# Low parts of the recurrence's weights, its query-decay products and partial sums of two norms: VectorE in place of GpSimd

## The chip, the cores and the metric

One core of a Trainium2 chip runs the whole program. The metric is the device time of one execution in microseconds (us); of several runs the median counts. Engines: PE is TensorE (matrix products, transposes), ACT is ScalarE, DVE is VectorE, POOL is GpSimd, SP issues most of the DMAs. Each engine works through its own instructions in program order, and waits on semaphores for what another engine makes.

## The reference

A streaming encoder with two layers: layer 0 has a pooling mixer, layer 1 an HGRN2 recurrence, and each is followed by a convolutional feed-forward network (FFN); a last norm ends it. It runs on a prompt of 1024 rows and on 64 rows of a running stream, with a width of 1024, 8 heads of 128 and an FFN width of 2816.

```python
def trunk(...):
    for i in range(DEPTH):                    # DEPTH = 2
        hn = rmsnorm(x, norm_mix_g[i])
        if i % 2 == 0: y, st = pool_mix(hn, ...)
        else:          y, st = hgrn_mix(hn, S0, w_in, lb, gn, w_out)
        x = x + y
        hn = rmsnorm(x, norm_ffn_g[i])
        y, cs = conv_ffn(hn, ...)             # w_up, 3-tap conv, silu(gate) * val, w_down
        x = x + y
    x = rmsnorm(x, norm_out_g)

# inside hgrn_mix, per head: zq, zf, zi, zg = split(h @ w_in)
q, k, log_f = silu(zq), (1 - lb) * sigmoid(-zf), ...     # f = exp(log_f), the decay per channel
S_new = exp(bC) * S + k_decayed^T v                      # state 128 x 128
o = (q * exp(b)) S + A v                                 # A: decayed q k products, causal
o = rmsnorm(o) * silu(zg);  y = o @ w_out
```

All of it is fp32.

## The kernel before, in words

**Layout.** The state x lies in SBUF with the 1024 channels as 8 tiles of 128 partitions, tokens along the free axis. The tokens are worked in three chunks of 384, 384 and 320 columns (256 of the prompt and the 64 of the other stream).

**Products.** An fp32 product is made of three passes of a rounded format (fp32r): hi times hi, hi times lo, lo times hi (`mm3`, L180 to L182). So each operand is split: the high part is a ScalarE cast, the low part is source minus high part, one `tensor_tensor` subtraction. For activations that is `split` (L185 ACT, L186 the engine that the caller names).

**Weights.** `load_ready` takes the next 128x512 block of a hand-written queue as soon as a slot of the weight pool is free: a DMA on SP's queue into one of the raw buffers, the ScalarE cast (L128) into `whi...`, the subtraction (L129, GpSimd) into `wlo...`. The phase in the queue is "f" for the FFNs and "g" for the recurrence; "g" has 64 blocks of w_in (`in`, head, projection, half) and 16 of w_out (`out`). Some of the blocks of "g" lie in a spare buffer that appears as `wx` in the trace. Blocks of the up projections are sums and differences of raw blocks, made on VectorE (L152).

**Norms.** `norm(c, gbase, nm, kind)` serves all of them: kind 0 is the norm ahead of FFN 0 (tiles `_x`), 1 the one ahead of the recurrence (`_m`), 2 the one ahead of FFN 1 (`_f`), 3 the last (`_o`). For each of the 8 channel tiles d ScalarE squares it; from d = 2 on the square is added to one of two partial sums, `acc0` for even d and `acc1` for odd d (L366). L373 adds the two, PE transposes (L378, `nps_`), VectorE reduces, `rstd` makes the reciprocal root by Newton steps on 128x3 values (L333 to L344, tile `nt_`), PE spreads it over the rows (L391, `nr_`), and per channel tile L417 scales and `split` makes `hnhi` and `hnlo`.

**Recurrence.** For each head and chunk four projections (`pj`, L180 to L182) make q, k and f, v, and the gate; `core` then makes qq = q times f (L915) and runs three levels of products over blocks of 4, 16 and 64 tokens: VectorE multiplies q and k by decays (L936, called at L938, L939 and L947 to L951), PE multiplies (L945, `pl`), VectorE copies under a mask into `at` (L960). Then come the states (L998), the head's norm and gate (tile `nt_g`), and the output projection `op`, which is added to x at L1049.

**Order.** PE's order is set by a hand-written scheduler in the kernel: tasks that are generators and yield the PE time and a latency (constants N_..., LAT_...). On the other engines the order follows from a list scheduler of the framework, which places instructions by its own estimate of when they are ready. Each engine then keeps that order.

Of the kernel before, what the change touches and what calls it, by code (L numbers as in the profile page):

```python
# [9 lines left out]
F32 = mybir.dt.float32  # L10
# [55 lines left out]
def trunk_kernel(ctx: ExitStack, tc: tile.TileContext, xtok, xs_tok, hist_tok, xf, par, gmix, pw, winm, ident_in,  # L66
# [39 lines left out]
    free = [(i, False) for i in range(NR)]  # L106
    extra_w = []

    def load_ready(most=None):

        while queue and (most is None or len(loaded) < most):
            ph, key, make = queue[0]
            own = [p for p in free if p[1]] if ph == "g" and key[:2] not in (("out", H - 2), ("out", H - 1)) else []
            p = own[0] if own else next((p for p in free if not p[1]), None)
            if p is None:
                return
            free.remove(p)
            queue.pop(0)
            places[key] = p
            i, extra = p  # L120
            nm = "_".join(str(k) for k in key)
            if extra:
                hi, lo = (extra_w[i // 2][:, (i % 2 * 2 + b) * HW_:(i % 2 * 2 + b + 1) * HW_] for b in range(2))
            else:
                hi = wp.tile([P, HW_], F32R, name=f"whi{nm}", tag=f"whi{i}", bufs=1)
                lo = wp.tile([P, HW_], F32R, name=f"wlo{nm}", tag=f"wlo{i}", bufs=1)
            src = make(nm)
            nc.scalar.copy(hi, src)  # L128
            nc.gpsimd.tensor_tensor(lo, src, hi.bitcast(F32), op=ALU.subtract)  # L129
            loaded[key] = (hi, lo)  # L130

    def raw_block(nm, src, i):
# [220 lines left out]
    def norm(c, gbase, nm, kind):  # L353
# [5 lines left out]
        for d in range(ND):  # L359
            a = acc[d % 2][:, :n]  # L360
            if d < 2:
                nc.scalar.activation(a, x[c][:, d, :], AF.Square)
            else:
                sq = slot(f"sq_{nm}{d}", *tags[2:])
                last = nc.scalar.activation(sq[:, :n], x[c][:, d, :], AF.Square)
                (nc.vector if kind == 0 or final and c == 2 or d % 2 else nc.gpsimd).tensor_tensor(a, a, sq[:, :n], op=ALU.add)  # L366
        if final:
            with tc.issue_after(last.ins):
                for d in range(ND):
# [31 lines left out]
        for d in range(ND):  # L401
            if final:
                on_pool = c < 2 or d in (2, 5)
                eng, r_ = (nc.gpsimd, rs) if on_pool else (nc.vector, pr)
                eng.tensor_tensor(x[c][:, d, :], x[c][:, d, :], r_[:, :n], op=ALU.mult)

                if c < 2 and d % 2 or c == 2 and (d % 2 == 0 or d == ND - 1):
                    d0 = d - (0 < d and (c < 2 or d % 2 == 0))
                    nc.sync.dma_start(y_out[c][:, d0:d + 1, :], x[c][:, d0:d + 1, :])
            else:  # L410
                if kind == 2 and c < 2 or kind == 0 and c == 1:
                    t = row(kind // 2, c, d)
                elif kind == 0 and c < 2:
                    t = slot(f"hn_{nm}{d}", ("hh1", "hl1")[d % 2], 2, F32, NMAX)
                else:
                    t = slot(f"hn_{nm}{d}", "cv", 3)
                last = nc.vector.scalar_tensor_tensor(t[:, :n], x[c][:, d, :], col(gbase, d), pr[:, :n], op0=ALU.mult, op1=ALU.mult)  # L417
                split(hn_hi[c][:, d, :], hn_lo[c][:, d, :], t[:, :n], (nc.vector, nc.gpsimd)[d % 2 and kind == 1])
                if d < ND - 1:
                    yield 0.0, N_STEP[kind]  # L420
        return last.ins
# [448 lines left out]
    def core(h, c, pr, stage):  # L870
# [41 lines left out]


        qq, q = qt[:, :n], qt[:, NMAX:NMAX + n]
        nc.gpsimd.tensor_tensor(qq, q, f[:, :n], op=ALU.mult)  # L915
        p0 = prod(kk, q, f"pl{nm}_d")
        nc.vector.tensor_tensor(at[:, :so].rearrange("p (b t) -> p b t", t=P), p0[:, :so].rearrange("p (b t) -> p b t", t=P),
                                ident.unsqueeze(1).to_broadcast([P, full, P]), op=ALU.mult)
# [261 lines left out]
```

## Time and profile before

| | |
|---|---|
| median of 3 runs | 2372.37 us (2372.25 to 2373.45) |
| the profiled execution | 2377.06 us |
| its span in the trace | 2375.2 us |
| mean granted PE clock over the span | 0.98 of full speed |

The profile is of one execution of its own, which took 4.7 us more than the median; its span is 1.9 us shorter than its time. Start times in rows count from the start of the span. FFN 0 ends at about 890 us, the recurrence runs from about 860 to 1580 us, FFN 1 begins at about 1525 us; the stretches overlap, since the three chunks follow one another.

### The profile page before, as it was taken

Reading aid. Unit: us, or ns where it says so; the run is one execution under the profiler, and the core shown is the slowest. Engines: PE = TensorE matmul, PEld = TensorE weight load, DVE = VectorE, ACT = ScalarE, POOL = GpSimd, SP = SyncE. Lnnn points to the kernel's source line nnn. Section 1 sums busy time; section 2 is a strip of 40 time slices with the busy share of each in tenths; the row PEclk is TensorE's granted clock in tenths of the full one; section 3 lists DMA queues with packets and bytes.
Section 4 is the critical chain, followed back from the end, with each engine's and each line's share of the span. In section 5 each row is a group of like instructions: output and inputs, shape, how many; then the busy total and the mean of one; then the engine's idle time right before and its main releaser. Section 6 shows DMA issues by size and latency. Waiting matters only on the chain. (4 is left out here: it accounts for less than half of the span.)

```text
span 2375.2 us, 38111 instructions
## 1 busy us (share of the span) xinstructions
PE 2284.7 (96%) x13830; PEld 2231.3 (94%) x13830; DVE 1613.8 (68%) x3728; ACT 904.3 (38%) x1965; POOL 1003.0 (42%) x1054
## 2 busy tenths in 40 slices
PE   9889999999999989999999999889999999999996
PEld 8889999999999989999999999878999999999996
DVE  6786656566666688767667767778766666666567
ACT  5444333334433353323323322345333333443335
POOL 1155554556655562112112211224454555564555
PEclk8999999999999999999999999989999999999998
DMA  7123333333433321001011000102343334433431
GB/s 233 49 81 116 125 121 120 123 125 129 138 116 125 124 69 36 26 18 54 26 35 40 32 26 22 36 25 76 111 130 116 125 119 134 134 124 117 129 120 76
DMA packets 118099, 218.70 MB, mean 92 GB/s; under 512 B 13436, under 2 KB 17404, under 8 KB 117528
## 3 DMA queue, kind: packets, MB, share of 16 engines
q1 hardware_dynamic: 117822, 216.15, 28.0%
q8 instruction: 109, 1.79, 0.3%
q14 instruction: 78, 0.64, 0.1%
q10 hardware_dynamic: 90, 0.12, 0.0%
HBM read 210.51 MB, written 5.72 MB: 91 GB/s over the span
## 5 line engine op out<-in xcount | busy, mean ns | idle before, releaser
L129 POOL TENSOR_TENSOR wloup_a<-rawup_a,whiup_a 128x512 fp32r<-128x512 f32 x368 | 513.1, 1411 | 568.1 <-ACT whiup_a L128 534.4
L128 ACT CAST whiup_a<-rawup_a 128x512 fp32r<-128x512 f32 x368 | 224.2, 617 | 573.8 <-PE dn L181 397.4
L152 DVE TENSOR_TENSOR rawup_a<-rawup_a,rawup_a 128x512 f32<-128x512 f32 x200 | 186.6, 933 | 286.4 <-DMA rawup_a<-w_up_in 261.4
L180 PE MATMUL dn<-hh,whidn 128*128 128x384 f32 (+1 forms) x1056 | 351.5, 333 | 11.5 <-DVE x L757 8.0
L181 PE MATMUL dn<-hl,whidn 128*128 128x384 f32 (+1 forms) x1056 | 348.7, 330 | 0.7 <-DVE hl L186 0.7
L182 PE MATMUL dn<-hh,wlodn 128*128 128x384 f32 (+1 forms) x1056 | 348.9, 330 | 0.0
L757 DVE TENSOR_TENSOR x<-x,dn 128x384 f32<-128x384 f32 (+1 forms) x528 | 262.3, 528 | 97.1 <-PE dn L182 95.5
L180 PEld LDWEIGHTS dn<-hh,whidn 128*128 128x128 f32 x1056 | 200.2, 190 | 18.0 <-DVE x L757 13.4
L181 PEld LDWEIGHTS dn<-hl,whidn 128*128 128x128 f32 x1056 | 200.1, 190 | 1.3 <-DVE hl L186 1.3
L182 PEld LDWEIGHTS dn<-hh,wlodn 128*128 128x128 f32 x1056 | 200.1, 189 | 0.0
L180 PE MATMUL pj<-hnhi,whiin 128*128 128x384 f32 (+1 forms) x528 | 185.0, 350 | 1.1 <-ACT hnhi L185 1.1
L181 PE MATMUL pj<-hnlo,whiin 128*128 128x384 f32 (+1 forms) x528 | 173.0, 328 | 2.4 <-POOL hnlo L186 2.4
L182 PE MATMUL pj<-hnhi,wloin 128*128 128x384 f32 (+1 forms) x528 | 173.2, 328 | 0.0
L630 DVE SCALAR_TENSOR_TENSOR cv<-ge,prm,cv 128x322 f32<-128x322 f32 (+1 forms) x132 | 132.1, 1002 | 48.2 <-ACT cv L629 42.0
L129 POOL TENSOR_TENSOR wlodn<-rawdn,whidn 128x512 fp32r<-128x512 f32 x88 | 119.0, 1354 | 100.9 <-ACT whidn L128 76.8
L960 DVE COPY_PREDICATED at<-masks,pl 128x64 f32<-128x64 uint8 (+7 forms) x432 | 117.0, 293 | 50.5 <-PE pl L945 48.8
L632 ACT ACTIVATE cv<-cv 128x322 f32<-128x322 f32 (+1 forms) x132 | 67.2, 509 | 161.3 <-DVE cv L631 160.9
L180 PE MATMUL pv<-hnhi,whiup_a 128*128 128x320 f32 (+1 forms) x384 | 122.1, 318 | 0.0
L180 PE MATMUL pg<-hnhi,whiup_a 128*128 128x320 f32 (+1 forms) x384 | 122.1, 318 | 0.0
L182 PE MATMUL pg<-hnhi,wloup_a 128*128 128x320 f32 (+1 forms) x384 | 121.7, 317 | 0.0
L182 PE MATMUL pv<-hnhi,wloup_a 128*128 128x320 f32 (+1 forms) x384 | 121.5, 317 | 0.0
L181 PE MATMUL pg<-hnlo,whiup_a 128*128 128x320 f32 (+1 forms) x384 | 121.5, 316 | 0.0
(1234 smaller groups left out, 6199.0 us busy)
## 6 DMA issues: line engine op xcount, KB each, us to landing
rawup_a<-w_up_in SPq DMA_DIRECT2D x568, 256.0 KB, 2.8
rawdn<-w_dn_in SPq DMA_DIRECT2D x88, 256.0 KB, 3.1
rawin<-w_in_in SPq DMA_DIRECT2D x64, 256.0 KB, 2.6
rawupp_a<-w_up_in SPq DMA_DIRECT2D x16, 256.0 KB, 2.7
rawout<-w_out_in SPq DMA_DIRECT2D x16, 256.0 KB, 2.7
xt<-xtok_in SPq DMA_DIRECT2D x7, 448.0 KB, 6.7
x<-xf_in SPq DMA_DIRECT2D x2, 1536.0 KB, 8.7
y_out<-x SPq DMA_DIRECT2D x8, 384.0 KB, 2.3
```

The costliest lines, as they stand in the source:

```text
L128: nc.scalar.copy(hi, src)
L129: nc.gpsimd.tensor_tensor(lo, src, hi.bitcast(F32), op=ALU.subtract)
L152: nc.vector.tensor_tensor(t[0], t[0], t[1], op=bs[2])
L180: nc.tensor.matmul(ps, w[0][:, wsl], a_hi, start=first, stop=False, skip_group_check=more)
L181: nc.tensor.matmul(ps, w[0][:, wsl], a_lo, start=False, stop=False, skip_group_check=more)
L182: nc.tensor.matmul(ps, w[1][:, wsl], a_hi, start=False, stop=last, skip_group_check=more)
L630: nc.vector.scalar_tensor_tensor(t[:, :wd], ge[:, 0:wd], prm[:, cw[0]:cw[0] + 1], t[:, :wd], op0=ALU.mult, op1=ALU.add)
L632: nc.scalar.activation(t[:, :wd], t[:, :wd], AF.Silu)
L757: nc.vector.tensor_tensor(x[c][:, d, :], x[c][:, d, :], pd[:, :n], op=ALU.add)
L960: nc.vector.copy_predicated(dst[:, :, :, d * hh:], mk, a)
```

## The change

Four kinds of GpSimd instructions become VectorE instructions, with the same operands:

- the low parts (L129) of the weights of phase "g", 80 subtractions of 128x512, by a new helper `lo_engine(ph, key)`;
- the even partial sums of the norms of kind 1 and 2 (L366), 18 additions; the last norm keeps 6 of its own on GpSimd;
- the low parts of the odd channel tiles of the norm of kind 1 (L418), 12 subtractions;
- qq (L915), 24 products.

```diff
--- before.py
+++ after.py
@@ -105,6 +105,9 @@
     places = {}
     free = [(i, False) for i in range(NR)]
     extra_w = []
+
+    def lo_engine(ph, key):
+        return nc.vector if ph == "g" else nc.gpsimd
 
     def load_ready(most=None):
 
@@ -126,7 +129,7 @@
                 lo = wp.tile([P, HW_], F32R, name=f"wlo{nm}", tag=f"wlo{i}", bufs=1)
             src = make(nm)
             nc.scalar.copy(hi, src)
-            nc.gpsimd.tensor_tensor(lo, src, hi.bitcast(F32), op=ALU.subtract)
+            lo_engine(ph, key).tensor_tensor(lo, src, hi.bitcast(F32), op=ALU.subtract)
             loaded[key] = (hi, lo)
 
     def raw_block(nm, src, i):
@@ -363,7 +366,7 @@
             else:
                 sq = slot(f"sq_{nm}{d}", *tags[2:])
                 last = nc.scalar.activation(sq[:, :n], x[c][:, d, :], AF.Square)
-                (nc.vector if kind == 0 or final and c == 2 or d % 2 else nc.gpsimd).tensor_tensor(a, a, sq[:, :n], op=ALU.add)
+                (nc.vector if kind < 3 or c == 2 or d % 2 else nc.gpsimd).tensor_tensor(a, a, sq[:, :n], op=ALU.add)
         if final:
             with tc.issue_after(last.ins):
                 for d in range(ND):
@@ -415,7 +418,7 @@
                 else:
                     t = slot(f"hn_{nm}{d}", "cv", 3)
                 last = nc.vector.scalar_tensor_tensor(t[:, :n], x[c][:, d, :], col(gbase, d), pr[:, :n], op0=ALU.mult, op1=ALU.mult)
-                split(hn_hi[c][:, d, :], hn_lo[c][:, d, :], t[:, :n], (nc.vector, nc.gpsimd)[d % 2 and kind == 1])
+                split(hn_hi[c][:, d, :], hn_lo[c][:, d, :], t[:, :n], nc.vector)
                 if d < ND - 1:
                     yield 0.0, N_STEP[kind]
         return last.ins
@@ -912,7 +915,7 @@
 
 
         qq, q = qt[:, :n], qt[:, NMAX:NMAX + n]
-        nc.gpsimd.tensor_tensor(qq, q, f[:, :n], op=ALU.mult)
+        nc.vector.tensor_tensor(qq, q, f[:, :n], op=ALU.mult)
         p0 = prod(kk, q, f"pl{nm}_d")
         nc.vector.tensor_tensor(at[:, :so].rearrange("p (b t) -> p b t", t=P), p0[:, :so].rearrange("p (b t) -> p b t", t=P),
                                 ident.unsqueeze(1).to_broadcast([P, full, P]), op=ALU.mult)
```

The order of PE's instructions is the same, row by row. VectorE has 134 rows of it more and GpSimd 134 fewer. The list scheduler also moves some of the other VectorE instructions. From L108 on a line of the changed kernel has a number that is 3 higher (L129 becomes L132, L186 becomes L189, L366 becomes L369, L417 becomes L420).

**At the border from FFN 0 to the recurrence.** VectorE before, around the norm of the second chunk; `nt_m` are the Newton steps, `hn_m` the scaled rows, `cv` and `hl` belong to FFN 0:

```order
L344 SCALAR_TENSOR_TENSOR nt_m_9105<-nt_m_9105 128x3
L186 TENSOR_TENSOR hl_20_2_9177<-hr_20_2_9173,hh_20_2_9176 128x320
L417 SCALAR_TENSOR_TENSOR hn_m_9213<-x_94,prm,nr_m_9209 128x384
L186 TENSOR_TENSOR hnlo_100<-hn_m_9213,hnhi_97 128x384
L417 SCALAR_TENSOR_TENSOR hn_m_9247<-x_94,prm,nr_m_9209 128x384
L417 SCALAR_TENSOR_TENSOR hn_m_9269<-x_94,prm,nr_m_9209 128x384
L630 SCALAR_TENSOR_TENSOR cv_21_2_9233<-ge_21_2_9226,prm,cv_21_2_9233 128x322
L631 SCALAR_TENSOR_TENSOR cv_21_2_9233<-ge_21_2_9226,prm,cv_21_2_9233 128x322
L186 TENSOR_TENSOR hnlo_100<-hn_m_9269,hnhi_97 128x384
```

GpSimd before, in the same place, where `wloin` and `wx` are low parts of weights of the recurrence:

```order
L129 TENSOR_TENSOR wloin_0_0_9195<-rawin_0_0_9196,whiin_0_0_9194 128x512
L129 TENSOR_TENSOR wx_9329<-rawin_2_0_9332,wx_9329 128x512
L129 TENSOR_TENSOR wloin_0_1_9221<-rawin_0_1_9222,whiin_0_1_9220 128x512
L624 COPY ncv_92<-ge_21_2_9226 128x2
L625 COPY ncv_92<-ge_21_2_9226 128x2
L129 TENSOR_TENSOR wx_9329<-rawin_2_1_9336,wx_9329 128x512
L129 TENSOR_TENSOR wloin_1_0_9255<-rawin_1_0_9256,whiin_1_0_9254 128x512
L186 TENSOR_TENSOR hnlo_100<-hn_m_9247,hnhi_97 128x384
L129 TENSOR_TENSOR wloin_1_1_9277<-rawin_1_1_9278,whiin_1_1_9276 128x512
L129 TENSOR_TENSOR wx_9330<-rawin_3_0_9340,wx_9330 128x512
```

VectorE of the changed kernel, in the same place:

```order
L347 SCALAR_TENSOR_TENSOR nt_m_9105<-nt_m_9105 128x3
L132 TENSOR_TENSOR wloin_0_0_9195<-rawin_0_0_9196,whiin_0_0_9194 128x512
L420 SCALAR_TENSOR_TENSOR hn_m_9213<-x_94,prm,nr_m_9209 128x384
L132 TENSOR_TENSOR wloin_0_1_9221<-rawin_0_1_9222,whiin_0_1_9220 128x512
L189 TENSOR_TENSOR hnlo_100<-hn_m_9213,hnhi_97 128x384
L420 SCALAR_TENSOR_TENSOR hn_m_9247<-x_94,prm,nr_m_9209 128x384
L420 SCALAR_TENSOR_TENSOR hn_m_9269<-x_94,prm,nr_m_9209 128x384
L633 SCALAR_TENSOR_TENSOR cv_21_2_9233<-ge_21_2_9226,prm,cv_21_2_9233 128x322
L189 TENSOR_TENSOR hnlo_100<-hn_m_9247,hnhi_97 128x384
L634 SCALAR_TENSOR_TENSOR cv_21_2_9233<-ge_21_2_9226,prm,cv_21_2_9233 128x322
L132 TENSOR_TENSOR wloin_1_0_9255<-rawin_1_0_9256,whiin_1_0_9254 128x512
L189 TENSOR_TENSOR hnlo_100<-hn_m_9269,hnhi_97 128x384
```

The low parts of the weights now stand between the Newton steps, the scaled rows and the low parts of the rows, and those of the odd rows stand behind their own L420 and no longer behind three subtractions of weights on GpSimd.

**In the second chunk's product levels.** VectorE before, head 2; `at` is the masked copy, `q` and `k` the level products (head 3's q is in the same queue under another number):

```order
L960 COPY_PREDICATED at_1_11673<-masks,pl_1_0_2_11700 128x32x3
L936 TENSOR_TENSOR q__11445<-q__11445,tp_1_11674 128x24x8
L960 COPY_PREDICATED at_1_11673<-masks,pl_1_0_2_11700 128x32x2
L936 TENSOR_TENSOR q__11445<-q__11445,tp_1_11674 128x24x4
L960 COPY_PREDICATED at_1_11673<-masks,pl_1_0_2_11700 128x32
L960 COPY_PREDICATED at_1_11673<-masks,pl_1_1_0_11757 128x16x12
L936 TENSOR_TENSOR q__11445<-q__11445,tp_1_11674 128x24x4 x3
L936 TENSOR_TENSOR k__11634<-k__11634,tp_1_11674 128x48x4
L960 COPY_PREDICATED at_1_11673<-masks,pl_1_1_0_11757 128x16x8
L936 TENSOR_TENSOR k__11634<-k__11634,tp_1_11674 128x24x8
```

And of the changed kernel:

```order
L963 COPY_PREDICATED at_1_11673<-masks,pl_1_0_2_11700 128x32x3
L939 TENSOR_TENSOR q__11445<-q__11445,tp_1_11674 128x24x8
L963 COPY_PREDICATED at_1_11673<-masks,pl_1_0_2_11700 128x32x2
L939 TENSOR_TENSOR q__11445<-q__11445,tp_1_11674 128x24x4
L963 COPY_PREDICATED at_1_11673<-masks,pl_1_0_2_11700 128x32
L132 TENSOR_TENSOR wloin_2_0_11772<-rawin_2_0_11773,whiin_2_0_11771 128x512
L963 COPY_PREDICATED at_1_11673<-masks,pl_1_1_0_11757 128x16x12
L939 TENSOR_TENSOR q__11445<-q__11445,tp_1_11674 128x24x4 x3
L939 TENSOR_TENSOR k__11634<-k__11634,tp_1_11674 128x48x4
L963 COPY_PREDICATED at_1_11673<-masks,pl_1_1_0_11757 128x16x8
L939 TENSOR_TENSOR k__11634<-k__11634,tp_1_11674 128x24x8
```

The subtraction for block 2_0 of w_in stands between two masked copies, behind the two q products of this level and ahead of the copies and products of the next.

**At the border from the recurrence to FFN 1.** VectorE before; `acc_f`, `sq_f` and `row1w` belong to the norm ahead of FFN 1, `states` and `nt_g` to the last head:

```order
L976 TENSOR_TENSOR k__16198<-k__16198,tp_2_16399 128x2x64
L366 TENSOR_TENSOR acc_f_16626<-acc_f_16626,sq_f_16632 128x384
L417 SCALAR_TENSOR_TENSOR row1w_16524<-x_94,prm,nr_f_16520 128x384
L366 TENSOR_TENSOR acc_f_16626<-acc_f_16626,sq_f_16638 128x384
L417 SCALAR_TENSOR_TENSOR row1w_16524<-x_94,prm,nr_f_16520 128x384
L366 TENSOR_TENSOR acc_f_16626<-acc_f_16626,sq_f_16644 128x384
L186 TENSOR_TENSOR hnlo_100<-row1w_16524,hnhi_97 128x384 x2
L417 SCALAR_TENSOR_TENSOR row1w_16575<-x_94,prm,nr_f_16520 128x384
L998 SCALAR_TENSOR_TENSOR states<-states,tp_2_16399,pu_2_16663 128x128
L417 SCALAR_TENSOR_TENSOR row1w_16575<-x_94,prm,nr_f_16520 128x384
L186 TENSOR_TENSOR hnlo_100<-row1w_16575,hnhi_97 128x384
L998 SCALAR_TENSOR_TENSOR states<-states,tp_2_16399,pu_2_16663 128x128
```

And of the changed kernel:

```order
L979 TENSOR_TENSOR k__16198<-k__16198,tp_2_16399 128x2x64
L369 TENSOR_TENSOR acc_f_16625<-acc_f_16625,sq_f_16629 128x384
L369 TENSOR_TENSOR acc_f_16626<-acc_f_16626,sq_f_16632 128x384
L369 TENSOR_TENSOR acc_f_16625<-acc_f_16625,sq_f_16635 128x384
L369 TENSOR_TENSOR acc_f_16626<-acc_f_16626,sq_f_16638 128x384
L369 TENSOR_TENSOR acc_f_16625<-acc_f_16625,sq_f_16641 128x384
L369 TENSOR_TENSOR acc_f_16626<-acc_f_16626,sq_f_16644 128x384
L420 SCALAR_TENSOR_TENSOR row1w_16524<-x_94,prm,nr_f_16520 128x384 x2
L420 SCALAR_TENSOR_TENSOR row1w_16575<-x_94,prm,nr_f_16520 128x384
L189 TENSOR_TENSOR hnlo_100<-row1w_16524,hnhi_97 128x384 x2
L189 TENSOR_TENSOR hnlo_100<-row1w_16575,hnhi_97 128x384
L1001 SCALAR_TENSOR_TENSOR states<-states,tp_2_16399,pu_2_16663 128x128
```

The six partial sums of the norm (three of them from GpSimd) now stand in a row, behind the k product of the last level and ahead of the four L420 rows, two of which stood between the sums before. Further on, L376, which adds the two partial sums, stands ahead of the first Newton step of the gate (L336) in place of behind it.

## Rows read from the trace of the kernel before

**Rows 1.** The page's first part: busy time, share of the span, instructions.

```profile
PE 2284.7 (96%) x13830; PEld 2231.3 (94%) x13830; DVE 1613.8 (68%) x3728; ACT 904.3 (38%) x1965; POOL 1003.0 (42%) x1054
```

**Rows 2.** Windows: length, busy time per engine, granted clock, DMA share, GB/s.

```profile
840.00:900.00 60.00, 50.55 (x283) 48.02 (x282) 52.12 (x122) 29.52 (x60) 35.41 (x31) 0.91 0.18 59
960.00:1020.00 60.00, 60.00 (x390) 58.15 (x389) 41.47 (x158) 18.48 (x56) 10.23 (x11) 1.00 0.08 26
1500.00:1560.00 60.00, 48.53 (x281) 44.41 (x279) 49.38 (x148) 23.17 (x56) 17.75 (x15) 0.89 0.12 36
1560.00:1620.00 60.00, 54.77 (x289) 52.18 (x290) 46.08 (x116) 27.69 (x61) 11.12 (x19) 0.89 0.09 29
1740.00:1800.00 60.00, 60.00 (x365) 60.00 (x364) 36.50 (x56) 25.42 (x50) 37.43 (x40) 1.00 0.40 130
```

**Rows 3.** Waits of PE, 840 to 1700 us: total, times, longest.

```profile
PE pl L945 <- DVE q__16127 L936: 7.3, 2, 3.9
PE nr_m L391 <- DVE nt_m L344: 3.5, 2, 2.3
PE pl L972 <- DVE k__16198 L936: 2.6, 1, 2.6
PE pj L181 <- POOL hnlo L186: 2.4, 1, 2.4
PE nps_f L378 <- DVE acc_f L373: 1.6, 1, 1.6
PE pl L945 <- DVE q__9504 L936: 1.6, 1, 1.6
PE pl L972 <- DVE k__14156 L936: 1.5, 1, 1.5
PE pl L945 <- DVE q__11445 L936: 1.3, 1, 1.3
```

**Rows 4.** Groups of GpSimd instructions, 840 to 1700 us: busy, mean ns, idle before.

```profile
L129 POOL TENSOR_TENSOR wloin<-rawin,whiin 128x512 fp32r<-128x512 f32 x44 | 58.1, 1324 | 111.1 <-ACT whiin L128 105.7 <-DVE at L960 3.1 <-DVE k__9766 L936 1.8
```

**Rows 5.** Timelines of GpSimd and VectorE in a head: start, length, instruction, idle before.

```profile
1091.00 1.26 POOL L129 TENSOR_TENSOR wloin<-rawin,whiin 128x512 fp32r<-128x512 f32 x1 [9.78 <-ACT whiin L128]
1091.08 1.29 DVE L936 TENSOR_TENSOR q__11445<-q__11445,tp 128x96 f32<-128x96 f32 x1
1063.19 0.25 DVE L936 TENSOR_TENSOR q__11132<-q__11132,tp 128x96 f32<-128x96 f32 x1
```

**Rows 6.** Timeline of VectorE at the start of FFN 1: three undisturbed instructions.

```profile
1580.87 0.55 DVE L186 TENSOR_TENSOR hnlo<-row1q,hnhi 128x384 fp32r<-128x384 f32 x1
...
1598.29 0.49 DVE L373 TENSOR_TENSOR acc_f<-acc_f,acc_f 128x320 f32<-128x320 f32 x1
1598.70 0.68 DVE L152 TENSOR_TENSOR rawup_a<-rawup_a,rawup_a 128x512 f32<-128x512 f32 x1
```

**Rows 7.** Timelines of VectorE and GpSimd, first border.

```profile
857.61 1.39 DVE L630 SCALAR_TENSOR_TENSOR cv<-ge,prm,cv 128x322 f32<-128x322 f32 x1 [0.54 <-ACT cv L629]
...
860.08 1.24 POOL L186 TENSOR_TENSOR hnlo<-hn_m,hnhi 128x384 fp32r<-128x384 f32 x1
...
864.38 1.25 DVE L334 TENSOR_SCALAR nt_m<-nt_m 128x3 int32<-128x3 int32 x1
...
872.32 0.90 DVE L343 TENSOR_TENSOR nt_m<-nt_m 128x3 f32<-128x3 f32 x1
...
892.52 0.95 DVE L343 TENSOR_TENSOR nt_m<-nt_m 128x3 f32<-128x3 f32 x1
```

**Rows 8.** Timelines of VectorE and GpSimd, last border.

```profile
1527.21 1.23 DVE L340 TENSOR_TENSOR nt_g<-nt_g 128x3 f32<-128x3 f32 x1
...
1550.93 1.00 POOL L366 TENSOR_TENSOR acc_f<-acc_f,sq_f 128x384 f32<-128x384 f32 x1 [11.73 <-ACT sq_f L365]
...
1551.08 1.26 DVE L186 TENSOR_TENSOR hnlo<-row1w,hnhi 128x384 fp32r<-128x384 f32 x1
...
1557.35 1.02 DVE L936 TENSOR_TENSOR k__16198<-k__16198,tp 128x160 f32<-128x160 f32 x1
```

## The prediction

> **What bounds the kernel now.** I read the page's busy times first [rows 1]: PE is busy in 96% of the span, GpSimd in 42%, VectorE in 68%. So the change takes work from an engine with room and gives it to one with less, and it can gain only where PE stands idle. The windows say where that is [rows 2]. In a window of FFN 1 (1740 to 1800 us) PE is busy for 60.00 of 60 us, in one inside the recurrence (960 to 1020 us) as well. At the two borders it isn't: 50.55 in 840 to 900 us, 48.53 in 1500 to 1560, 54.77 in 1560 to 1620. In the first two of these VectorE is busy for 52.12 and 49.38 us, and the granted clock is 0.91 and 0.89. The waits of PE between 840 and 1700 us [rows 3] name VectorE nearly everywhere: level products (q, k), Newton steps (nt_m), the last sum of a norm (acc_f); one is for a low part from GpSimd (2.4 us). Nothing outside this stretch has an edited instruction in front of a waiting PE.
>
> The reader is to see next why VectorE is late. In head 1 of the second chunk a product of 128x96 takes 1.29 us where the same product in the head before takes 0.25 [rows 5]; the long one starts 0.08 us after a GpSimd subtraction of 1.26 us and ends with it. So a VectorE instruction that meets a GpSimd subtraction lasts as long as that subtraction. The same holds at the borders: a Newton step on 128x3 takes 1.25, 0.90 and 0.95 us [rows 7] and 1.23 [rows 8], a low part of 128x384 1.26 [rows 8] where 0.55 is its undisturbed time [rows 6]. GpSimd's work does not run beside VectorE's at these places; it holds it up.
>
> The Trainium skill, "SBUF — State Buffer", section "Who interferes with whom", says that a VectorE instruction with two SBUF inputs contends with a GpSimd instruction that reads SBUF, and that one with a single SBUF input outside the two-port modes does not. The trace agrees for the products; L334 with its one input, 1.25 us, would have to be in such a mode, which no row here shows. Were single-input steps not freed, place 1 below would keep 1.1 us more.
>
> **The price on VectorE.** A subtraction of 128x512 lasts 0.68 us, one of 128x384 0.55 [rows 6]. Instructions overlap in the pipeline: the 0.49 us sum at 1598.29 has a successor at 1598.70, 0.08 us before its end [rows 6]. So each costs the engine about 0.60, 0.47 and 0.41 us. The moved work is 80 x 0.60 + (12 + 18 + 24) x 0.47 = 73 us, against some 1.3 us each on GpSimd for the subtractions of weights [rows 4]. VectorE's busy time grows by these 73 less the stretches that go. The trace doesn't show these subtractions on VectorE; bounds are 0.55 (the 128x384 row) and 0.68.
>
> **Place 1, the border from FFN 0 (850 to 895 us).** Six Newton steps from 864.38 to 872.32 us sum to 5.2 us (the first and the last of them are in [rows 7]); undisturbed ones in the same chain take 0.16, so 4.2 us of stretch. Other VectorE rows that met GpSimd, from 857.61 to 892.52 us (nine; 1.39 and 0.95 the outermost), hold another 7.5 us. Given back: 11.7 us. Added in the same stretch: 12 subtractions of weights x 0.60, 8 of rows x 0.47, 3 sums x 0.41, one qq, together 12.7 us. So VectorE is as full as it was. What changes is the order. The odd rows' low part no longer stands behind the subtractions of weights on GpSimd (1.24 us long, at 860.08, and PE waited 2.4 us for one of them) [rows 3, 7]; in VectorE's order it stands behind its own scaled row and another row's, and one subtraction of a weight (0.60) ahead. I take 1.5 us off that wait. Of the 3.5 us of waits for nt_m I take 1.5 off: the chain loses 4.2 us of stretch, but subtractions of weights and rows (four to six at 0.5) come between its steps. Against it, 1.0 for the weights that now stand ahead of the even rows' low parts, of which PE takes one each 0.9 us or so. Sum -2.0; bounds -7.0 (both waits go) and +1.0 (only the new work counts).
>
> **Place 2, the heads (900 to 1500 us).** Three even heads of the second chunk have the collision of [rows 5] with a PE wait of 1.3 us each behind it (q__11445, and two more like it) [rows 3]. 1.04 us of each is stretch: 1.29 less 0.25. In the changed order the subtraction stands behind the q products, so PE gets them in time: -3.1 us. The wait for k__14156, 1.5 us [rows 3], ends 1.0 earlier by the same reason. The 68 other subtractions and 24 qq of the recurrence lie in windows where PE has no idle time and VectorE 18 us in 60 [rows 2]; they cost nothing while that room lasts. If the cover is gone, one subtraction costs PE its 0.60 us. In front of the next level's chain stands one in each of some 7 heads: bounds 0 and 4.2, I take +1.0, near the lower end, as the level chains ran without a PE wait in most heads with stretches of 1.04 in them. Sum -3.1.
>
> **Place 3, the border to FFN 1 (1522 to 1572 us).** Of five stretched gate steps, 1.23 us the longest [rows 8], three lay under sums on GpSimd and become short: taken at 0.9, as the last two of [rows 7], less 0.16, that is 2.2 us. Two lay under subtractions for FFN 1, which stay on GpSimd. Three sums of 0.47 are added on VectorE: -0.8. For k__16198 PE waits 2.6 us [rows 3]; the chain had three stretches of 0.7 us (1551.08, 1557.35, and one between) [rows 8], and the sums now stand behind it: -2.1 at best, but the masked copies and output projections around it arrive by PE's own pace, so I take -1.1. For the norm's final sum PE waits 1.6 us [rows 3]; it moves ahead of the gate's steps: -1.2. The six sums in a row wait for ScalarE's squares, and the scaled rows behind them: +0.5, bounds 0 and 2.5. Sum -2.6. The largest wait, 7.3 us for q__16127 [rows 3], is mostly the chain of the last head and has nothing left to hide it; I leave it but for the -0.8.
>
> **Sum.** -2.0 - 3.1 - 2.6 = -7.7 us. Against the profiled execution of 2377.1 us that is 2369.4; that run stood 4.7 us above the median of 2372.4, so by the median the forecast is 2364.7 us. PE's half-clock stretches are taken as they are.
>
> **Rivals.**
> - *VectorE waits for ScalarE (slower).* VectorE works in order. On GpSimd the subtractions waited 105.7 us in all for ScalarE's casts, 2.4 us each over 44 [rows 4], and nothing stood behind them. On VectorE such a wait holds the level products behind it. The casts wait in turn for a slot that PE frees. Where the list scheduler put a subtraction too early, PE loses about 1.3 us, as it now does behind a stretched q [rows 3]. Six of the 80 cancel the gain (6 x 1.3 = 7.8); twelve give 2364.7 + 15.6 = 2380. For it: 2.4 us of wait per subtraction. Against it: in the one place looked at closely, the subtraction stands behind the products that PE waits for, and the cast is done long before (GpSimd ran it 9.78 us after its last work, at once when the cast ended [rows 5], in a stretch without haste for the weight).
> - *The exchange comes out even (no change).* VectorE's stretches go and its own work fills the same time: 11.7 against 12.7 us at place 1. Then only the heads gain, and place 1 and place 3 give nothing: -3.1 and +1 or so, 2370 to 2374. The Trainium skill, "Perfetto Trace Analysis", section "Optimizing Scalar/DVE Operations", has it this way: GpSimd and VectorE share a read port, so moving work between them might not help. By that rule the time would stay at about 2372.
> - *The clock gains too.* At the borders the granted clock was 0.91, 0.89 and 0.89 over 60 us each [rows 2]: 0.09, 0.11 and 0.11 of 60 are 18.6 us of full-speed time lost. PE's idle time preceded the stretches at half clock in the trace. If shorter waits remove half of it, another 9 us go: 2355.
> - *It isn't done.* Excluded by the order, which has the rows on VectorE.
>
> **How the numbers follow.** The forecast has 0.47 (about 2360 to 2369), the exchange that comes out even 0.22, VectorE waiting for ScalarE 0.15, the clock 0.16. A measurement of this kernel tells about 0.2%, 4.7 us, from no change: 2367.6 is the bound. The forecast lies 3 us past it; a tenth of it and the larger part of the even exchange fall within. So faster: 0.60; same: 0.25; slower: 0.15. The range holds the forecast, nearly all of the even exchange and the nearer half of the clock: 2355 to 2374.
>
> **What would show it.** After: DVE busy about 1600 to 1620 us, GpSimd some 175 less; in the heads no q product of 1.29 us and the three waits near 0.3; no wait of PE for a low part from GpSimd; Newton steps of nt_m near 0.16. It is wrong if waits of PE for q or k grow in the heads and VectorE's idle time before a subtraction of a weight is put down to the cast, or if the clock at the borders leaves the present 0.89 to 0.91.

## The result and the profile after

| | before | changed |
|---|---|---|
| median of 5 runs | 2373.32 us (2372.25 to 2375.55) | 2359.53 us (2352.71 to 2363.22) |
| profiled execution | 2377.06 us | 2355.90 us |
| its span, granted clock | 2375.2 us, 0.981 | 2353.8 us, 0.986 |

The changed kernel is faster: ratio 0.9936, 95% interval 0.9921 to 0.9951, 13.8 us by the medians. The forecast was 7.7 us. The two profiled executions are 21.2 us apart, more than the medians: that of the kernel before lies 3.7 us above its median, and the changed kernel's five executions spread over 10 us, the shorter ones with the higher granted clock (0.982 to 0.986). Of all executions below, one of e5 took 6704 us and is left out.

The first part of the page of the changed kernel answers to [rows 1]. VectorE has only 7 us more busy time, with 134 instructions more, and GpSimd has 159 us less:

```profile
PE 2275.5 (97%) x13830; PEld 2225.6 (95%) x13830; DVE 1620.8 (69%) x3862; ACT 903.2 (38%) x1965; POOL 844.4 (36%) x920
```

Where the time went is seen in windows that begin and end at the same places of PE's program in both kernels: the first border, the heads, the last border, the start of FFN 1. Kernel before (length, busy time of PE, PEld, DVE, ACT and POOL, granted clock, DMA share, GB/s):

```profile
847.00:897.00 50.00, 40.55 (x222) 38.09 (x221) 43.73 (x100) 25.50 (x52) 32.62 (x28) 0.90 0.22 70
897.00:1510.00 613.00, 606.27 (x3833) 579.68 (x3833) 423.95 (x1591) 187.33 (x532) 115.04 (x115) 1.00 0.10 32
1510.00:1617.00 107.00, 90.36 (x485) 83.88 (x484) 83.99 (x228) 44.64 (x103) 25.84 (x32) 0.87 0.10 32
1617.00:1717.00 100.00, 92.04 (x539) 88.56 (x539) 78.92 (x122) 43.62 (x89) 53.60 (x52) 0.97 0.32 105
```

Changed kernel, the same four:

```profile
845.70:893.70 48.00, 38.80 (x223) 37.42 (x222) 44.03 (x125) 24.69 (x52) 2.10 (x3) 0.93 0.22 73
893.70:1501.00 607.30, 605.73 (x3834) 579.80 (x3834) 432.80 (x1686) 187.61 (x532) 2.22 (x22) 1.00 0.10 32
1501.00:1599.50 98.50, 84.77 (x484) 79.51 (x483) 81.51 (x237) 44.30 (x103) 13.65 (x20) 0.93 0.11 34
1599.50:1699.40 99.90, 91.93 (x539) 88.42 (x538) 79.95 (x122) 43.57 (x89) 53.54 (x52) 0.97 0.33 105
```

Length less PE's busy time is PE's idle time: 9.45 to 9.20 us at the first border, 6.73 to 1.57 in the heads, 16.64 to 13.73 at the last border, 7.96 to 7.97 after it. That is 0.25 + 5.16 + 2.91 = 8.3 us less idle time. The windows are 16.3 us shorter in all; the other 8.0 us are PE's busy time for the same instructions (829.22 to 821.23). Most of it lies at the two borders, 1.8 and 5.6 us, where the granted clock rose from 0.90 to 0.93 and from 0.87 to 0.93. The remaining 5.1 us between the two spans lie outside these windows, 1.3 ahead of them and 3.8 behind, where no edited instruction stands in front of a waiting PE; I count them as scatter of two single executions.

PE's waits in the changed kernel, 840 to 1700 us, answer to [rows 3]:

```profile
PE pl L948 <- DVE q__16127 L939: 7.5, 2, 4.6
PE dn L183 <- DVE x L760: 5.6, 3, 3.7
...
PE nps_m L381 <- DVE ss_m L385: 1.7, 1, 1.7
PE dn L183 <- ACT hh L188: 1.7, 1, 1.7
PE nr_m L394 <- DVE nt_m L347: 1.5, 1, 1.5
PE pl L975 <- DVE k__16198 L939: 1.4, 1, 1.4
...
PE pl L948 <- DVE q__11445 L939: 0.3, 1, 0.3
```

The wait for GpSimd's hnlo is gone, those for nt_m, k__16198 and q__11445 are shorter, acc_f and k__14156 no longer appear. New are a wait of 3.7 us for a residual sum of FFN 0 (x, L760), the longest of three, one of 1.7 for the norm's sums (ss_m) and one of 1.7 for a ScalarE cast of FFN 0 (hh).

In head 1 of the second chunk, the place of [rows 5], VectorE's timeline now shows the q product at its undisturbed length, and the subtraction of the weight behind it and behind one more masked copy; PE waits 0.31 us where it waited 1.3:

```profile
1088.03 0.26 DVE L939 TENSOR_TENSOR q__11445<-q__11445,tp 128x96 f32<-128x96 f32 x1
1088.23 0.30 DVE L963 COPY_PREDICATED at<-masks,pl 128x32 f32<-128x32 uint8 x1
1088.34 0.71 DVE L132 TENSOR_TENSOR wloin<-rawin,whiin 128x512 fp32r<-128x512 f32 x1
```

At the first border, VectorE's and PE's timelines show the new wait. Three subtractions of weights in a row, 1.9 us, stand ahead of the residual sum that PE waits for; a fourth and two low parts of rows stand ahead of these:

```profile
867.02 1.89 DVE L132 TENSOR_TENSOR wx<-rawin,wx 128x512 fp32r<-128x512 f32 x3
868.82 0.48 DVE L760 TENSOR_TENSOR x<-x,dn 128x320 f32<-128x320 f32 x1
869.36 0.41 PE L183 MATMUL dn<-hh,whidn 128*128 128x320 f32 x1 [3.74 <-DVE x L760]
```

At the last border, VectorE's and GpSimd's timelines show that steps of the gate are still stretched, by subtractions for FFN 1 that stay on GpSimd:

```profile
1515.89 1.27 DVE L341 TENSOR_TENSOR nt_g<-nt_g 128x3 f32<-128x3 f32 x1
...
1518.82 1.59 POOL L132 TENSOR_TENSOR wloup_a<-rawup_a,whiup_a 128x512 fp32r<-128x512 f32 x1 [1.69 <-ACT whiup_a L131]
1519.17 1.28 DVE L345 TENSOR_SCALAR nt_g<-nt_g 128x3 f32<-128x3 f32 x1
```

### The profile page after: what moved, and what is told of

It is laid out like the page before. It is cut to its first block, busy times and chain, and to the rows that moved or that the text cites. A ratio compares the mean times of both kernels' runs of the same rounds, so it can differ in the third digit from the quotient of the medians.

```text
span 2353.8 us, 38047 instructions
## 1 busy us (share of the span) xinstructions
PE 2275.5 (97%) x13830; PEld 2225.6 (95%) x13830; DVE 1620.8 (69%) x3862; ACT 903.2 (38%) x1965; POOL 844.4 (36%) x920
## 5 line engine op out<-in xcount | busy, mean ns | idle before, releaser
L132 POOL TENSOR_TENSOR wloup_a<-rawup_a,whiup_a 128x512 fp32r<-128x512 f32 x368 | 518.0, 1424 | 592.2 <-ACT whiup_a L131 552.5
L760 DVE TENSOR_TENSOR x<-x,dn 128x384 f32<-128x384 f32 (+1 forms) x528 | 262.2, 528 | 96.1 <-PE dn L185 95.1
L132 POOL TENSOR_TENSOR wlodn<-rawdn,whidn 128x512 fp32r<-128x512 f32 x88 | 119.1, 1355 | 100.1 <-ACT whidn L131 81.3
L184 PE MATMUL pv<-hnlo,whiup_a 128*128 128x320 f32 (+1 forms) x384 | 121.5, 317 | 0.0
```

What stands on the lines that cost most here:

```text
L132: lo_engine(ph, key).tensor_tensor(lo, src, hi.bitcast(F32), op=ALU.subtract)
L184: nc.tensor.matmul(ps, w[0][:, wsl], a_lo, start=False, stop=False, skip_group_check=more)
L760: nc.vector.tensor_tensor(x[c][:, d, :], x[c][:, d, :], pd[:, :n], op=ALU.add)
```

## The experiments

Every kernel was timed in five rounds; ratios are to the kernel before on the same chip, whose medians there are 2373.2 to 2374.5 us. The changed kernel was timed only with the result, so differences to it are of medians from different chips; by the ratios they come out up to 3.5 us otherwise. The diffs are against the changed kernel unless said otherwise, and show the edited lines alone.

**Each half of the change alone.** The first run moves only the weights' subtractions, the second only the rest.

```diff
 e1_lo_only
-(nc.vector if kind < 3 or c == 2 or d % 2 else nc.gpsimd)
+(nc.vector if kind == 0 or final and c == 2 or d % 2 else nc.gpsimd)
-split(..., t[:, :n], nc.vector)
+split(..., t[:, :n], (nc.vector, nc.gpsimd)[d % 2 and kind == 1])
-nc.vector.tensor_tensor(qq, ...)
+nc.gpsimd.tensor_tensor(qq, ...)
 e2_rest_only
-        return nc.vector if ph == "g" else nc.gpsimd
+        return nc.gpsimd
```

> Only the low parts of the recurrence's weights go to VectorE; the sums, the odd low parts of rows and qq stay on GpSimd. Theory A (a VectorE instruction that meets a GpSimd subtraction is held up as long as that one runs, and the gain is what is no longer held up): the heads give all of their part, about 5.5 us by the trace after; the two borders keep GpSimd's sums and low parts of rows of about 1 us each and give half of theirs, so 2363 to 2367 us. Theory B (the gain is that low parts are made in 0.6 us and not in 1.3 us behind a queue, wherever GpSimd's other work stands): all but a little of the gain, 2359 to 2362. Theory C (the gain is PE's clock at the borders, the rest comes out even): near the kernel before, 2368 to 2373, with the granted clock at 0.981.

Measured: 2366.81 us, ratio 0.9964 (0.9950 to 0.9977).

> The sums, the odd low parts of rows and qq on VectorE; the low parts of the recurrence's weights stay on GpSimd. Theory A: the three waits of 1.3 us for q in the second chunk's heads stay, since their q products still meet a subtraction of a weight; the last border gives its part, the first one little: 2364 to 2369. Theory B: the weights' subtractions were what was late, so 2369 to 2373. Theory C: where the last border's clock gains, 2364 to 2369 too; its mark is a granted clock above 0.981 with the waits elsewhere as before.

Measured: 2368.15 us, ratio 0.9972 (0.9959 to 0.9984). Both are as theory A has it; the two gains, 7.7 and 6.3 us, add up to about the whole 13.8. For e2 theory C had the same range, but there PE's idle time at the last border fell as well, from 16.6 to 13.3 us, with the waits for acc_f and k__16198 as in the changed kernel. With the weights' subtractions back on GpSimd the three waits for q are back, at 1.3 us in PE's list of waits; with only the weights moved they are at 0.3, and PE runs through the heads as in the changed kernel. So the heads belong to the weights, and qq and the norms give nothing there. The other profiles agree: in the heads, between the same instructions of PE as in the windows above, it idles 5.1 to 6.9 us in the four kernels where GpSimd makes a subtraction per weight (before, e2, e3, e5), and 1.0 to 1.6 us in the seven where GpSimd makes none or, in e10, four, and VectorE has no ghost (changed, e1, e4, e6, e7, e10, e11).

**The hold-up without the dependency.** The changed kernel with a subtraction on GpSimd that nothing reads.

```diff
 e3_ghost, in load_ready
+            if ph == "g" and ghost:
+                nc.gpsimd.tensor_tensor(ghost[0], src[:, :NMAX], hi.bitcast(F32)[:, :NMAX], op=ALU.subtract)
 in hgrn_start
+        ghost.append(room("ghost", "x"))
```

> The changed kernel with its VectorE order, and on GpSimd a second subtraction of 128x384 of the same operands behind each cast of 76 of the 80 weights of the recurrence; its result goes to a tile that nothing reads, so that nothing waits for GpSimd. Theory A: the stretches of VectorE come back and the moved work stays on it, so the gain of the heads and of the first border is lost, at least 7 us: 2367 to 2378, with q products of 1 us and waits of PE of 1 us or more in the heads. Theory B: low parts are as early as in the changed kernel, 2359 to 2362. Theory C: between, by the clock: 2359 to 2366.

Measured: 2367.83 us, ratio 0.9964 (0.9951 to 0.9977). Theory B falls: no instruction waits for these subtractions, the low parts are made on VectorE, and 8 us of the gain are lost. The rows of PE, VectorE and ScalarE stand in the same order as in the changed kernel, every one, so the order on VectorE is no rival here; its busy time is 1649.7 us, 28.9 more for the same instructions. In its profile PE idles 5.1 us in the heads, where it idles 1.6 in the changed kernel, and 10.4 against 9.2 at the first border. The timelines of GpSimd, VectorE and PE show the picture of [rows 5] again, in the same head:

```profile
1095.38 1.00 POOL L135 TENSOR_TENSOR ghost<-rawin,whiin 128x384 f32<-128x384 f32 x1 [11.86 <-ACT whiin L132]
1095.41 1.08 DVE L943 TENSOR_TENSOR q__11470<-q__11470,tp 128x96 f32<-128x96 f32 x1
1096.64 1.05 PE L952 MATMUL pl<-q__11470,k__11663 128*128 128x192 f32 x5 [1.13 <-DVE q__11470 L943]
```

**What of GpSimd's work it is.** A memset in place of the ghost subtraction.

```diff
 e6_memset, in load_ready
+            if ph == "g" and ghost:
+                nc.scalar.copy(ghost[0][:, :1], hi.bitcast(F32)[:, :1])
+                nc.gpsimd.memset(ghost[0], 0.0)
```

> The changed kernel, and on GpSimd a memset of 128x384 behind each cast of 76 of the recurrence's weights, tied to the cast by a copy of one column on ScalarE; nothing waits for it. The subtraction in this place gave back 8 us of the gain. If what holds VectorE up is that GpSimd reads SBUF: no stretched product, 2358 to 2362. If any work of GpSimd does it: q products as long as the memset, 2363 to 2368.

Measured: 2357.24 us, ratio 0.9941 (0.9926 to 0.9956), the changed kernel's own gain. A memset takes 0.42 us, less than a subtraction, so its price could only have been smaller; but GpSimd's and VectorE's timelines show that a two-input subtraction which starts inside one isn't held up at all (0.69 us, as undisturbed). So it is for all 65 subtractions of weights that meet a memset (at most 0.71 us):

```profile
1259.70 0.42 POOL L136 MEMSET ghost<- 128x384 f32 x1 [1.79 <-ACT ghost L135]
1259.80 0.69 DVE L133 TENSOR_TENSOR wloout<-rawout,whiout 128x512 fp32r<-128x512 f32 x1
```

The Trainium skill, "SBUF — State Buffer", section "Who interferes with whom", says this: a VectorE instruction with two SBUF inputs contends with a GpSimd instruction that reads SBUF and not with one that only writes it. The run agrees, with 0.69 us beside the memset.

**The price of VectorE's own work.** The ghost subtraction on VectorE, whole and half.

```diff
 e8_vector_ghost, in load_ready (e9_half_ghost: 192 columns in place of NMAX = 384)
+            if ph == "g" and ghost:
+                nc.vector.tensor_tensor(ghost[0], src[:, :NMAX], hi.bitcast(F32)[:, :NMAX], op=ALU.subtract)
```

> The changed kernel, with the subtraction of 128x384 that nothing reads on VectorE in place of GpSimd: 76 x 0.47 = 36 us more work on VectorE, none on GpSimd. Theory A (VectorE's own work costs nothing where PE has the lead; only the borders are full): 1 to 4 us at the first border, nothing in the heads, 2360 to 2364. The even exchange (VectorE's own work fills the time that the stretches gave back): the heads lose as with GpSimd's, 2365 to 2372.

Measured: 2380.91 us, ratio 1.0032 (1.0022 to 1.0042), 21 us over the changed kernel. Both expectations fail; VectorE's work is not free in the heads. VectorE's timeline shows why: between one masked copy and the q product that PE waits for stand two subtractions of weights, a ghost, a product of the next q and work on the output, and PE waits 2.3 us for the q product at 1004.75. It waits as long for three more q products, and 1.1 us each for those of four other heads.

```profile
1001.31 0.69 DVE L133 TENSOR_TENSOR wloin<-rawin,whiin 128x512 fp32r<-128x512 f32 x1
1001.92 0.55 DVE L135 TENSOR_TENSOR ghost<-rawin,whiin 128x384 f32<-128x384 f32 x1
1002.39 0.48 DVE L854 TENSOR_TENSOR q__10790<-q__10790,pj 128x320 f32<-128x320 f32 x1
1002.79 0.61 DVE L1040 SCALAR_TENSOR_TENSOR ogr<-pto,prm,gt__10477 128x384 f32<-128x384 f32 x1
...
1003.68 0.68 DVE L133 TENSOR_TENSOR wloin<-rawin,whiin 128x512 fp32r<-128x512 f32 x1
1004.28 0.55 DVE L192 TENSOR_TENSOR ogl<-ogr,ogh 128x384 fp32r<-128x384 f32 x1
1004.75 0.25 DVE L943 TENSOR_TENSOR q__10530<-q__10530,tp 128x96 f32<-128x96 f32 x1
1005.15 1.22 PE L952 MATMUL pl<-q__10530,k__10589 128*128 128x192 f32 x6 [2.29 <-DVE q__10530 L943]
```

VectorE's busy time is 30.5 us over the changed kernel's, about as much as the 28.9 of e3, which cost 8 us. So the amount alone does not give the price.

> The changed kernel, with a subtraction of 128x192 that nothing reads on VectorE behind each of 76 low parts: half the columns of the one that made it 21 us slower. By the trace's durations of some 0.27 us in a row each, 20 us of work in place of 36. If VectorE's own work has a price per us wherever it is put (0.6 us per us, as 21 for 36): 2369 to 2374. If the price comes from where the list scheduler put it (level chains with more than about 1 us of slack cost nothing): well under half, 2360 to 2366.

Measured: 2366.61 us, ratio 0.9968 (0.9959 to 0.9978), 7 us over the changed kernel. VectorE's busy time is 17.4 us over the changed kernel's, less than the 20 that were expected, as e8's 30.5 are less than 36. That is 0.4 us per us against 0.7: no fixed price, and not small either; it lies between the two readings. How much of it is load and how much the place where the list scheduler put it stays open, since its order moves with the ghost's size.

**The last border.** Only the 9 even sums of the norm ahead of FFN 1 on VectorE, then all but these.

```diff
 e5_sums2_only, against the kernel before
-(nc.vector if kind == 0 or final and c == 2 or d % 2 else nc.gpsimd)
+(nc.vector if kind in (0, 2) or final and c == 2 or d % 2 else nc.gpsimd)
 e11_sums2_back
-(nc.vector if kind < 3 or c == 2 or d % 2 else nc.gpsimd)
+(nc.vector if kind < 2 or final and c == 2 or d % 2 else nc.gpsimd)
```

> The kernel before, with only the 9 even sums of the norm ahead of FFN 1 on VectorE. The runs so far leave two readings of the last border. Theory A (what GpSimd holds up there are the gate's Newton steps and the k products that met these sums): they alone give the last border's part, of which the trace after shows 8.7 us against the kernel before: 2364 to 2368. Rival D (the weights' subtractions that are still on GpSimd there must go as well): no more than 3 us, 2370 to 2374. The predicted term of the last border was 2.6 us, 2371.

Measured: 2368.6 us, the median of eight executions, ratio 0.9983 (0.9970 to 0.9995).

> The changed kernel, with only the 9 even sums of the norm ahead of FFN 1 back on GpSimd. Moved alone they gave 4 us. If the parts add up: 2362 to 2365. If at the last border they are worth more with the weights gone from GpSimd (the run with only the weights moved had 7.9 us more than the changed kernel between 1507 and 1630 us): 2366 to 2369.

Measured: 2365.07 us, ratio 0.9971 (0.9955 to 0.9986). By the medians the sums give 4.7 us when moved alone, between the two readings, and cost 5.5 when taken back, at the upper edge of the range in which the parts add up. By the ratios they give 4 and cost 8, each with an interval of 3 to 5 us either way, so the times don't settle whether the parts add up. The profiles do better: the last border takes 107.1 us in the kernel before and 100.0 in e5, 98.7 in the changed kernel and 105.1 in e11. That is 7.1 and 6.4 us, alike with the weights on GpSimd and on VectorE. So nine additions of 128x384 or 128x320 are worth about a third of the whole gain, and nothing shows that it hangs on the weights being gone as well.

**Better versions.** The four subtractions that still stretch the gate's steps go to VectorE; then the recurrence's norm goes back to GpSimd as well, where VectorE is full; then four weights of head 0 too.

```diff
 e4_first4 (nfirst counts the up projection's blocks of FFN 1)
-        return nc.vector if ph == "g" else nc.gpsimd
+        if ph == "f" and key[1] == 1 and key[0] == "up":
+            nfirst[0] += 1
+        return nc.vector if ph == "g" or 0 < nfirst[0] <= 4 else nc.gpsimd
 e7_mix, beside e4's lines
-(nc.vector if kind < 3 or c == 2 or d % 2 else nc.gpsimd)
+(nc.vector if kind in (0, 2) or final and c == 2 or d % 2 else nc.gpsimd)
-split(..., t[:, :n], nc.vector)
+split(..., t[:, :n], (nc.vector, nc.gpsimd)[d % 2 and kind == 1])
 e10_mix2, beside e7's lines
+        if key[:3] in (("in", 0, 2), ("in", 0, 3)):
+            return nc.gpsimd
```

> The changed kernel, with the first four low parts of FFN 1's weights on VectorE too (they are the four GpSimd subtractions that the trace after has between 1515 and 1527 us, over the gate's Newton steps). Theory A: four stretched steps of some 1.1 us each go, 4 x 0.6 us of subtractions come: 2356 to 2359. Theory B: the low parts are needed much later, no change: 2359 to 2361. Theory C: shorter waits at the last border bring the clock up as well: 2352 to 2357, granted clock 0.985 or more.

Measured: 2358.65 us, ratio 0.9927 (0.9911 to 0.9943).

> The changed kernel, with the even sums and the odd low parts of rows of the recurrence's norm on GpSimd as before, and the first four low parts of FFN 1's weights on VectorE. By the traces so far the first border is 1.3 us shorter with these sums and low parts on GpSimd, and the last one up to 3.5 us shorter with those four on VectorE. Theory A with VectorE full at the first border: 2355 to 2358.5. If the first border's difference is not theirs: 2358 to 2361.

Measured: 2354.43 us, ratio 0.9918 (0.9905 to 0.9930).

> The mixed kernel (even sums and odd low parts of the recurrence's norm on GpSimd, first four low parts of FFN 1 on VectorE), and the four low parts of head 0's third and fourth projection on GpSimd as before. In the trace of the mixed kernel three of them stand on VectorE in front of a residual sum of FFN 0 for which PE waits 2.3 us. If that is what the wait hangs on: 1 to 2 us less, 2352 to 2354. If GpSimd holds the Newton steps there for as long: no change, 2354 to 2357.

Measured: 2354.61 us, ratio 0.9919 (0.9906 to 0.9932). The first can't be told from the changed kernel. In its profile, though, the last border takes 95.2 us against 98.7, and 96.4 and 96.3 in the other two, so the four subtractions are worth some 2 to 3.5 us there. The mixed ones are the fastest kernels measured, 18.8 and 19.5 us under the kernel before on their chips; against the changed kernel (0.9936) they are 5 us better by the medians, with intervals that overlap. In PE's waits of e7, up to 900 us, the new wait is down from 3.7 to 2.3 us, that for nt_m from 1.5 to 1.2, and the one for ss_m, 1.7 us, is gone, while 0.7 us for GpSimd's hnlo and 0.6 for a cast of a row (hnhi) come in:

```profile
PE dn L186 <- DVE x L763: 2.3, 1, 2.3
PE dn L186 <- ACT hh L191: 1.3, 1, 1.3
PE nr_m L397 <- DVE nt_m L350: 1.2, 1, 1.2
```

The four weights of e10 make no further difference, as its second reading had it: the longest wait for x falls from 2.3 to 1.0 us, but those for nt_m grow from 1.2 to 2.5 in all and that for hh from 1.3 to 3.0. Whether the recurrence's norm is better on GpSimd is thus indicated, not shown: PE idles 7.8 us (e7) and 9.8 (e10) in the first border and the heads together, against 10.7 in e4, but the times of e7 and e4 have intervals that overlap.

## Why the prediction was right, and where it was off

**The mechanism held.** PE waited for VectorE instructions that GpSimd's subtractions held up: the ghost subtraction, for which nothing waits, brings them back with every row of PE, VectorE and ScalarE in the same order.

**The sum was of PE's idle time, and that came out: 7.7 us forecast, 8.3 in the profile.** Its three terms did not come out one by one:

- *Place 1* was set at 2.0 us and gave 0.25. The step that failed is the charge of 1.0 us against 1.5 off nt_m and 1.5 off hnlo. Both waits did fall (3.5 to 1.5 us, 2.4 to none), and 2.7 us for hnhi and q__9504 went that were not in the sum. But against these 7.1 us the moved work brought 7.1 of new waits: 3.7 for a residual sum of FFN 0, an instruction that the argument had not looked at, 1.7 for ss_m and 1.7 for hh. The residual sum is late behind either half of the change, 2.9 us in e1 and 2.6 in e2. Here the even exchange of the second rival is what happened, as its 11.7 against 12.7 us said (of the 11.7, the 7.5 of other stretches come to 7.0 by the trace).
- *Place 2* was set at 3.1 us and gave 5.2. The charge of 1.0 us for subtractions ahead of a level's chain did not come. The wait for k__14156 went as a whole (1.5 us, 1.0 taken), as did three waits of some 0.35 us for totals (tp, L910) that were not in the sum.
- *Place 3* was set at 2.6 us and gave 2.9: the wait for k__16198 fell by 1.2 us (1.1 taken), that for acc_f by 1.6 (1.2 taken). The 7.3 us for q__16127 stayed, at 7.5; the 0.8 taken off there did not come.

**What was left out was the clock, and how much of the median it makes stays open.** The forecast took PE's half-clock stretches as they are. In the profiled pair PE's busy time for the same work fell by 8.0 us, about as much again as the waits. The median moved 13.8 us, 5.5 more than the idle time.

The last border's part of this repeats. Between the same instructions of PE in every profile, its busy time there is 89.0 to 90.5 us in the three kernels with FFN 1's even sums on GpSimd (before, e1, e11), 86.9 to 88.6 in e2, e3, e5 and e9, and 84.2 to 85.3 in the other six; its idle time is 16.1 to 16.7 us in the first group and 11.0 to 13.7 in the others. So the clock there goes with the change, though not by idle time alone: 13.1 to 13.3 us of it go with 86.9 to 88.6, and 13.7 with 85.0 to 85.3.

The first border's part does not repeat: PE's busy time there is 37.5 us in e2 and 40.6 in e7, without regard to the edit. And ahead of it, where no edit makes PE wait, PE's busy time for the same instructions lies between 814.5 us (e7) and 825.4 (e3). So single executions of these kernels differ by up to 11 us there that belong to no edit, and their mean granted clock with them.

Over all runs that mean is 0.9817 for the kernel before (51 runs) and 0.9840 for the changed one (5 runs), and the changed kernel's own runs go from 2363.2 and 2359.5 us at 0.982 to 2355.9 and 2352.7 at 0.986. But at 0.982 the kernel before has a median of 2373.6 us (20 runs), so 10 to 14 us lie between the two kernels at one clock too, more than the 8.3. The third rival had 9 us for the clock and 0.16 of the chance; what happened is the forecast with a part of that rival on top. The sum gave 2364.7 us; the other 5 us to the measured 2359.5 come from no term of it, and it is the range, drawn wide for this rival, that covers them.

**The slower rival did not occur.** VectorE waited for a ScalarE cast ahead of a weight's subtraction for 6.0 us in all (3.6 for wloin, 1.7 for wx, 0.7 for wloout), against 105.7 us for wloin alone on GpSimd [rows 4]; no wait of PE for VectorE after 840 us has one in the 5 us ahead of it. But e8 shows another way to a slower kernel: 30.5 us more of VectorE's own work, with no more waits for casts (5.8 us), and it is slower than before.

**The marks.** VectorE's busy time is 1620.8 us (1600 to 1620 forecast), GpSimd's 159 less (175), q products are at 0.26 us, the steps of nt_m at 0.15 to 0.16 but for one of 1.26 at 848.59, which met a subtraction for FFN 0. One sign of being wrong came: the clock at the borders left 0.89 to 0.91. In the windows of [rows 2], which hold somewhat later work of the changed kernel, it has 0.94, 0.91 and 0.97:

```profile
840.00:900.00 60.00, 50.80 (x295) 49.08 (x294) 54.17 (x158) 29.13 (x61) 2.10 (x3) 0.94 0.18 58
1500.00:1560.00 60.00, 49.31 (x284) 45.21 (x283) 49.80 (x168) 23.06 (x62) 6.01 (x5) 0.91 0.09 29
1560.00:1620.00 60.00, 54.34 (x324) 52.68 (x322) 53.21 (x105) 34.22 (x70) 18.38 (x25) 0.97 0.17 50
```

That is the clock that the sum took as given.

## What to carry to other kernels

Before moving work to an idle engine, or leaving it there, look at what its instructions do to the lengths of another engine's: the same instruction at 0.25 and at 1.29 us in one trace is a hold-up that no list of waits names. Moving the work to the engine that was held up pays where the moved instructions stand behind what PE waits for, and gives nothing where that engine is full; so decide it place by place (here: the weights and FFN 1's norm on VectorE, and, as far as the runs indicate, the recurrence's norm on GpSimd). And where PE idles and its granted clock is below 1, count the clock as a term of its own: here, at the last border, PE's busy time fell by 5.6 us beside 2.9 us of idle time.

## What the runs showed of the hardware

A GpSimd subtraction holds up VectorE by what both read, not by its being there. Products with two SBUF inputs wait for its end (0.25 to 1.29 us), and so does a TENSOR_SCALAR with one (1.28 us at 1519.17, ending with the GpSimd subtraction beside it). Instructions that read one input from PSUM run beside it at their usual length; in the kernel before, GpSimd's and VectorE's timelines show both kinds beside two subtractions:

```profile
1067.94 2.54 POOL L129 TENSOR_TENSOR wx<-rawin,wx 128x512 fp32r<-128x512 f32 x2 [18.69 <-ACT wx L128]
...
1069.59 0.49 DVE L1049 TENSOR_TENSOR x<-x,op 128x320 f32<-128x320 f32 x1
1070.08 0.61 DVE L975 TENSOR_TENSOR q__11132<-q__11132,tp 128x192 f32<-128x192 f32 x1
```

The sum at 1069.59, which reads `op` from PSUM, takes 0.49 us inside the two subtractions; the product of two SBUF tiles behind it, 0.35 us when undisturbed, takes 0.61 and ends 0.2 us after them. All 114 residual sums of FFN blocks (L757) that meet a GpSimd subtraction or sum in the kernel before take at most 0.56 us, as they do alone. For the single-input TENSOR_SCALAR the prediction had left open whether it is freed too; it is held up like the products, so the steps that became short belong to the gain. The Trainium skill, "SBUF — State Buffer", section "Who interferes with whom", allows for that: it lists tensor_scalar among the operations that can enter a two-port mode and then contend; the 1.28 us agree.
